# The ConvFFN of a hybrid decoder step in one pass, and in two passes with block products

## The chip, the cores and the metric

The kernel runs on one core of one Trainium2 chip. Time is device time in microseconds (us) of one execution. The core has five engines that work side by side, each through its own queue in order: TensorE (PE; its weight loads appear as PEld), VectorE (DVE), ScalarE (ACT), GpSimd (POOL) and SyncE (SP), which here issues nearly all DMA transfers. Working memory is SBUF, matmuls write into PSUM banks of 128 x 512 numbers, and large arrays lie in DRAM.

## What is computed

One layer of a decoder for 1024 prompt tokens and 8 x 8 sample tokens, in 32-bit floats, model width 1024. Attention of two kinds comes first; its output goes through W_o and is added to the residual h. Then comes the part that the change is about:

```python
def conv_ffn(n, prev, lw):                      # n = rmsnorm(h, g_ffn)
    a = n @ lw['ffn_w_gate']                    # 1024 x 2816
    c = n @ lw['ffn_w_up']                      # 1024 x 2816
    full = jnp.concatenate([prev, a], axis=1)   # two earlier rows
    conv = lw['ffn_conv_b'] + sum(w[j] * full[:, j:j + T] for j in range(3))
    y = (jax.nn.silu(conv) * c) @ lw['ffn_w_down']
    return y, full[:, -2:]
# h = h + y; then h = h + (p @ ple_w_proj) * sigmoid(rmsnorm(h, g_ple) @ ple_w_gate)
```

## The kernel before

Every product of 32-bit numbers is made of three matmuls (mm3): each operand is split into a high part (a cast on ScalarE) and a low part (a subtraction, on VectorE or GpSimd), and high x high, low x high and high x low are summed in PSUM. The helper for the split is at lines 115 to 117, for the three matmuls at lines 136 to 139, so many rows of the profile carry these line numbers.

A planner orders the instructions of each engine when the program is built. It takes them by their place in the source, but lets one that it thinks is ready go ahead of one that waits for data or for a free buffer. So instructions of a later place in the code can run early. Once the program is built the order on each engine is fixed.

Up to the FFN the work is a mixture of the prompt's dense stages and a stream over the sample's paged cache; wo_prompt (lines 1459 to 1484) starts the W_o product and loads the residual h (128 x 8 x 1024 in SBUF, 4 MB), and what is left of it follows at lines 1652 to 1662. There each token tile of 128 rows is normalised into a tile of its own (row_scale, xnorm, xn_tile), transposed by TensorE through PSUM and split into the tiles xg, in three groups of 384, 384 and 320 columns (256 prompt tokens and the 64 of the sample).

The FFN (lines 1682 to 1692) takes the 2816 columns in 22 chunks of 128, two at a time. ff_chunk multiplies the gate and the up weights of a chunk with all tokens: for each of the three groups of tokens 8 x 3 matmuls per matrix, with the activations moving (384, 384 and 320 columns). Then it copies the gate out of PSUM, runs the convolution on VectorE (lines 1597 to 1601), Silu on ScalarE, multiplies with up, and splits the result into sh and sl. After two chunks, down (lines 1380 to 1394) multiplies them with w_down for each token tile and adds the 512-column sums from PSUM to h in SBUF; down_sample (lines 1396 to 1408) does the same for the sample's 64 rows, whose high and low parts stand side by side in one 128-column operand. So h stays in SBUF for all of the FFN, and the product of gate and up never leaves SBUF.

During the last two chunks the tiles of h are normalised and transposed again (renormer), and the last stage (ple_unit, ple_sample) multiplies them with ple_w_gate and p with ple_w_proj, and writes the output.

## Time and profile before

| | us |
|---|---|
| median of 3 runs | 2309.12 |
| lowest, highest | 2305.56, 2311.49 |
| profiled execution, its own time | 2306.51 |
| its span (first to last instruction) | 2304.7 |
| TensorE busy | 2204.7 |
| VectorE busy | 1459.7 |
| ScalarE busy | 1243.1 |
| GpSimd busy | 951.0 |

The profile is that of the one execution that the last six rows tell of. Its page gives the busy time of each engine, then the span in 40 slices with the busy share of each in tenths, then the chain of work that ended last, and the costliest groups of instructions: line, engine, operation, written and read tiles, shape, count, then the group's busy time, the mean of one in ns, and the idle time of the engine before them with what ended it. In the table of stretches each engine has its busy time in the stretch, followed by the mean granted clock of TensorE, the DMA engines' busy share and GB/s. In the timeline a row has its start, its duration, engine, line and operation. Matmuls overlap each other, so their pace is read from the distance between starts, not from their durations.

### The profile page before, as it was taken

What the parts mean: (1) busy time and instruction counts of PE and PEld (TensorE: products, weight loads), DVE (VectorE), ACT (ScalarE), POOL (GpSimd) and SP (SyncE); (2) the same over time, 40 slices, a digit from 0 to 9 for tenths busy, and PEclk for the clock granted to TensorE, in tenths of its full rate; (3) what the DMA queues carried; (4) which work ended last, traced back from release to release, by engine and by line L of the source; (5) the groups of instructions that cost most, each with busy time, mean ns of one, the idle gap of its engine ahead of it and who ended that gap; (6) DMA issues with size and microseconds to landing.
All of it is one profiled execution on the core that took longest, in us unless ns stands there. A gap on an engine that the chain in (4) does not pass through costs nothing.

```text
span 2304.7 us, 37775 instructions
## 1 busy us (share of the span) xinstructions
PE 2204.7 (96%) x13855; PEld 1997.9 (87%) x13855; DVE 1459.7 (63%) x2386; ACT 1243.1 (54%) x3506; POOL 951.0 (41%) x1131
## 2 busy tenths in 40 slices
PE   7999999999999999998999869999999999999999
PEld 6889888878878888887887759999999999999999
DVE  4675775577798888887778665454444454444652
ACT  5666676777788888888557753221122221221531
POOL 5675677666777777776334540000000000000200
PEclk9899999999999999999999979999999999999999
DMA  5342334413242222215221112111111111111031
GB/s 179 118 133 94 103 111 145 125 49 104 73 112 64 59 64 63 58 43 174 78 68 61 46 33 78 46 46 43 32 55 47 46 46 37 46 47 32 29 116 40
DMA packets 173995, 169.84 MB, mean 74 GB/s; under 512 B 39022, under 2 KB 142931, under 8 KB 173811
## 3 DMA queue, kind: packets, MB, share of 16 engines
q1 hardware_dynamic: 161523, 125.47, 18.2%
q0 software_dynamic: 12288, 41.95, 5.9%
q8 instruction: 111, 1.82, 0.3%
q14 instruction: 73, 0.60, 0.1%
HBM read 140.81 MB, written 26.53 MB: 73 GB/s over the span
## 4 chain that ended last, share of the span: by engine, by line
PE 78%; ACT 7%; DVE 6%; POOL 3%; DMA 3%; issue 2%; SPq 0%; POOLq 0%; ACTq 0%; DVEq 0%
PE ps_gu L137 7%; PE ps_gu L139 7%; PE ps_gu L138 7%; PE ps_dn L137 5%; PE ps_dn L139 5%; PE ps_dn L138 5%; PE ks L137 4%; PE ks L139 4%; PE ks L138 4%; PE cpv L605 2%; ACT csq L542 2%; PE ctp L518 2%; PE ps_lt L276 2%; PE ps_pj L137 2%; DVE css L547 1%
## 5 line engine op out<-in xcount | busy, mean ns | idle before, releaser
L542 ACT ACTIVATE csq<-ks 128x256 f32<-128x256 f32 x1040 | 391.2, 400 | 103.0 <-PE ks L139 96.2
L547 DVE TENSOR_REDUCE css<-csq 128x16 f32<-128x1024 f32 (+1 forms) x264 | 315.9, 1197 | 70.8 <-ACT csq L542 67.8
L137 PE MATMUL ps_gu<-xh,guh 128*128 128x384 f32 (+1 forms) x1056 | 344.2, 326 | 0.9 <-ACT a L1591 0.7
L138 PE MATMUL ps_gu<-xl,guh 128*128 128x384 f32 (+1 forms) x1056 | 344.4, 326 | 0.0
L139 PE MATMUL ps_gu<-xh,gul 128*128 128x384 f32 (+1 forms) x1056 | 344.3, 326 | 0.0
L1391 DVE TENSOR_TENSOR h<-h,ps_dn 128x512 f32<-128x512 f32 x240 | 157.0, 684 | 88.8 <-PE ps_dn L139 88.4
L137 PEld LDWEIGHTS ps_gu<-xh,guh 128*128 128x128 f32 x1056 | 198.1, 188 | 1.8 <-ACT a L1591 0.8
L138 PEld LDWEIGHTS ps_gu<-xl,guh 128*128 128x128 f32 x1056 | 198.2, 188 | 0.5
L139 PEld LDWEIGHTS ps_gu<-xh,gul 128*128 128x128 f32 x1056 | 198.2, 188 | 0.0
L1602 POOL COPY cout<-a 128x2 f32<-128x2 f32 x22 | 11.1, 506 | 451.4 <-ACT a L1591 451.4
L137 PE MATMUL ps_dn<-wdh,sh 128*128 128x512 f32 x480 | 188.8, 396 | 1.6 <-DVE h L1391 0.9
L138 PE MATMUL ps_dn<-wdl,sh 128*128 128x512 f32 x480 | 188.0, 392 | 0.4 <-DVE wdl L117 0.4
L137 PE MATMUL ks<-mv1h,cTh 128*128 128x320 f32 (+1 forms) x520 | 168.4, 327 | 13.6 <-ACT cTh L116 7.0
L574 POOL TENSOR_TENSOR chl<-craw,chl 128x1024 fp32r<-128x1024 f32 x64 | 141.8, 2216 | 94.0 <-ACT chl L573 86.9
L139 PE MATMUL ps_dn<-wdh,sl 128*128 128x512 f32 x480 | 179.0, 391 | 0.0
L137 PE MATMUL ks<-mv0h,cTh 128*128 128x320 f32 (+1 forms) x520 | 169.3, 329 | 10.0 <-ACT csq L542 4.4
L116 ACT CAST guh<-stg 128x512 fp32r<-128x512 f32 x104 | 61.2, 620 | 174.1 <-PE ps_gu L138 136.6
L138 PE MATMUL ks<-mv1l,cTh 128*128 128x320 f32 (+1 forms) x520 | 152.4, 296 | 0.0
L138 PE MATMUL ks<-mv0l,cTh 128*128 128x320 f32 (+1 forms) x520 | 151.7, 294 | 0.0
L139 PE MATMUL ks<-mv1h,cTl 128*128 128x320 f32 (+1 forms) x520 | 143.9, 299 | 3.9 <-DVE cTl L117 3.9
L139 PE MATMUL ks<-mv0h,cTl 128*128 128x320 f32 (+1 forms) x520 | 145.0, 298 | 2.8 <-DVE cTl L117 2.7
L117 DVE TENSOR_TENSOR gul<-stg,guh 128x512 fp32r<-128x512 f32 x100 | 66.8, 696 | 121.0 <-ACT guh L116 120.5
(562 smaller groups left out, 6280.7 us busy)
## 6 DMA issues: line engine op xcount, KB each, us to landing
stage<-w_in SPq DMA_DIRECT2D x48, 256.0 KB
stg<-ffn_w_gate SPq DMA_DIRECT2D x44, 256.0 KB
stg<-ffn_w_up SPq DMA_DIRECT2D x44, 256.0 KB
stage<-ffn_w_down SPq DMA_DIRECT2D x44, 256.0 KB
oraw<-doT SPq DMA_DIRECT2D x16, 256.0 KB
stage<-w_o SPq DMA_DIRECT2D x16, 256.0 KB
h<-x_prompt SPq DMA_DIRECT2D x8, 512.0 KB
stg<-ple_w_gate SPq DMA_DIRECT2D x16, 256.0 KB
```

The costliest lines, as they stand in the source:

```text
L116: act.copy(hi, src)
L117: (lo_eng or dve).tensor_tensor(lo, src, hi.bitcast(F32), ALU.subtract)
L137: pe.matmul(ps, ah, bh, start=first, stop=False)
L138: pe.matmul(ps, ah, bl, start=False, stop=False)
L139: pe.matmul(ps, al, bh, start=False, stop=last)
L276: pe.matmul(ps, x, w, start=first, stop=last)
L518: pe.transpose(tp[:, i, :], craw[:, i, :], ident)
L542: act.activation(sq[:, f * 256:f * 256 + 256], ks[:, 0:256], AF.Square)
L547: dve.tensor_reduce(o.ss[:, g0 + i + 1 - n:g0 + i + 1, :].rearrange("p i h -> p (i h)"), sq2[:, :n].rearrange("p i (h n) -> p (i h) n", n= ...
L574: pool.tensor_tensor(ch[:, c0:c1, 128:256], src, ch[:, c0:c1, 0:128].bitcast(F32), ALU.subtract)
L605: pe.matmul(pv[:, 0:258], phl[:, i, :], o.ch[:, i, :], start=i == 0, stop=i == nt - 1)
L1391: dve.tensor_tensor(h[:, t, cs], h[:, t, cs], ps, ALU.add)
```

## The change

The FFN becomes two passes. In the first, all 22 chunks of gate, up, convolution and Silu are computed, and each chunk's product is written to DRAM (ds, 22 x 512 KB). In the second, the products come back as halves of 512 tokens, w_down as halves of 512 columns, and down adds to h by quarters. h itself is written to DRAM before it is normalised in place (dh, 4 MB) and loaded again between the passes. Its SBUF place is used by the first pass.

The first 768 tokens go another way through gate and up. Their transposed activations are four blocks: tokens 0 to 383 and 384 to 767, by the two halves of the 1024 inputs. The weights of a chunk are four blocks as well: gate and up, by the same halves (g0, g1, u0, u1). The eight block products that the gate and up of these tokens need are made out of seven products of sums and differences of blocks, as in Strassen's scheme: the activations' differences t1 to t4 are made once (turned_pair, from token tiles t and t + 3), the weights' s1 to s4 for each chunk (ff_weights, on GpSimd), and the seven products are put together by additions on VectorE and GpSimd in ff_chunk. The other 256 prompt tokens and the sample (320 columns) are multiplied as before, with the blocks g0, g1, u0, u1 (rest).

The sample's down is summed over all 22 chunks in two PSUM banks (acc_s) during the first pass, one chunk late, with w_down loaded and split for it there (sample_rows), and is added to the sample's residual once, between the passes. Pools of SBUF are opened and closed for each pass; the last stage's operands (p's slices, ple_w_proj) get a pool of their own, opened after the second pass.

The diff, cut to its core:

```diff
...
+    NP = 384
+    NR = T - 2 * NP + R
+    rx = opened("xhl", side="right")
+    xr = [z["xhl"].tile([P, 8, NR], F32R, name=f"xr{s}") for s in "hl"]
+    xb = {nm: [z["xhl"].tile([P, 4, NP], F32R, name=f"x{nm}{s}") for s in "hl"]
+          for nm in ("11", "21", "22", "t1", "t2", "t3", "t4")}
+    dh = [dram.tile([P if t < NT else R, D], F32, name=f"dh{t}") for t in range(NT + 1)]
+    ds = [dram.tile([P, T], F32, name=f"ds{f}") for f in range(NF)]
+
+    def normed(t):
+
+        row_scale(t)
+        x = hrows(t)
+        sp.dma_start(dh[t], x)
+        xnorm(t, x, pool if VIAP >> t & 1 else dve)
+
...
+    def turned_pair(t):
+        pc = slice(t * P, (t + 1) * P)
+        pt = {}
+        for nm, bank, rows, k0 in (("11", p2t, t, 0), ("12", pm, t + 3, 0), ("22", pm, t + 3, 4), ("21", p2t, t, 4)):
+            pt[nm] = bank([P, 4, P], "pt")
+            for k in range(4):
+                pe.transpose(pt[nm][:, k], hrows(rows)[:, (k0 + k) * P:(k0 + k + 1) * P], ident)
+        def quarter(tt, f):
+            return hrows(tt)[:, f * 512:f * 512 + 512].rearrange("p (k n) -> p k n", n=P)
+        def put(nm, src, eng):
+            split(*(x[:, :, pc] for x in xb[nm]), src, eng)
+        b11, t1, t2, t3 = quarter(t, 0), quarter(t, 1), quarter(t + 3, 0), quarter(t + 3, 1)
+        act.copy(b11, pt["11"])
+        dve.tensor_tensor(t1, pt["12"], b11, ALU.subtract)
+        dve.tensor_tensor(t2, pt["22"], t1, ALU.subtract)
+        put("22", pt["22"], dve)
+        put("11", b11, pool)
+        put("21", pt["21"], dve)
+        pool.tensor_tensor(t3, t2, b11, ALU.subtract)
+        dve.tensor_tensor(b11, pt["21"], t2, ALU.subtract)
+        put("t2", t2, pool)
+        put("t1", t1, dve)
+        put("t3", t3, pool)
+        put("t4", b11, dve)
+    def wstage():
+        return z["fw"].tile([P, 4, P], F32, tag="st", name="st", bufs=8)
+    def block(src, lo_eng):
+        hl = [z["fw"].tile([P, 4, P], F32R, tag="w" + s, name="w" + s, bufs=NWB) for s in "hl"]
+        split(*hl, src, lo_eng)
+        return hl
+    def ff_weights(f):
+        fs = slice(f * P, (f + 1) * P)
+        raw = []
+        for nm in ("ffn_w_gate", "ffn_w_up"):
+            for i in range(2):
+                r = wstage()
+                sp.dma_start(r, A[nm][0][i * 512:(i + 1) * 512, fs].rearrange("(k p) c -> p k c", p=P))
+                raw.append(r)
+        g0, g1, u0, u1 = raw
+        s1, s2, s3, s4 = (wstage() for _ in range(4))
+        w = wgu[f] = {}
+        w["g0"] = block(g0, dve)
+        w["g1"] = block(g1, dve)
+        pool.tensor_tensor(s1, u0, u1, ALU.add)
+        pool.tensor_tensor(s2, s1, g0, ALU.subtract)
+        w["s2"] = block(s2, dve)
+        w["s1"] = block(s1, dve)
+        pool.tensor_tensor(s4, g1, s2, ALU.subtract)
+        w["s4"] = block(s4, dve)
+        pool.tensor_tensor(s3, g0, u0, ALU.subtract)
+        w["s3"] = block(s3, dve)
+        w["u1"] = block(u1, pool)
+        w["u0"] = block(u0, pool)
+    def rest(w, names, bank):
+        ps = bank([P, 512], "ps_gu")
+        for i, nm in enumerate(names):
+            for k in range(4):
+                mm3(ps[:, :NR], w[nm][0][:, k], w[nm][1][:, k], xr[0][:, 4 * i + k], xr[1][:, 4 * i + k],
+                    i == k == 0, i == 1 and k == 3)
+        return ps
...
+    def sample_rows(f, half):
+        ss_ = chunks[f]
+        cs = slice(half * 512, half * 512 + 512)
+        raw = wstage().rearrange("p a b -> p (a b)")
+        sp.dma_start(raw, A["ffn_w_down"][0][f * P:(f + 1) * P, cs])
+        wd = [z["tp"].tile([P, 512], F32R, tag="wd" + s, name="wd" + s, bufs=2) for s in "hl"]
+        split(*wd, raw, dve)
+        if f == 0:
+            acc_s.append(p2t([P, 512], "ps_ds"))
+        for i in range(2):
+            pe.matmul(acc_s[half], ss_, wd[i], start=f == 0 and i == 0, stop=f == NF - 1 and i == 1)
+    def ff_chunk(f):
+        tp = z["tp"]
+        w = wgu.pop(f)
...
+        def product(wn, xn):
+            ps = both([P, 512], "ps_gu")[:, :NP]
+            for k in range(4):
+                mm3(ps, w[wn][0][:, k], w[wn][1][:, k], xb[xn][0][:, k], xb[xn][1][:, k], k == 0, k == 3)
+            return ps
+        pool.memset(a[:, 0:2], 0.0)
+        pool.tensor_copy(a_s[:, :, 0:2], prv[:, f])
+        m1, m2 = product("g0", "11"), product("g1", "21")
+        v, q, m5c = tmp("v"), tmp("q"), tmp("m5")
+        act.copy(v, m1)
+        dve.tensor_tensor(a[:, 2:2 + NP], m2, v, ALU.add)
+        pg = rest(w, ("g0", "g1"), both)
+        act.copy(a[:, 2 + 2 * NP:2 + T], pg[:, :T - 2 * NP])
+        act.copy(a_s[:, :, 2:10], pg[:, T - 2 * NP:NR].rearrange("p (b t) -> p b t", t=8))
+        if f + 1 < NF:
+            ff_weights(f + 1)
+        conv(0, NP)
+        act.activation(cv[:, 0:NP], cv[:, 0:NP], AF.Silu)
+        m6 = product("s2", "t2")
+        dve.tensor_tensor(v, m6, v, ALU.add)
+        if late:
+            sample_rows(late[0], 0)
+        m5 = product("s1", "t1")
+        act.copy(m5c, m5)
+        dve.tensor_tensor(q, m5, v, ALU.add)
+        m3 = product("s4", "22")
+        dve.tensor_tensor(a[:, 2 + NP:2 + 2 * NP], m3, q, ALU.add)
+        m7 = product("s3", "t3")
+        dve.tensor_tensor(v, m7, v, ALU.add)
+        pool.tensor_tensor(m5c, m5c, v, ALU.add)
+        if late:
+            sample_rows(late.pop(0), 1)
+        m4 = product("u1", "t4")
+        dve.tensor_tensor(v, m4, v, ALU.add)
+        pu = rest(w, ("u0", "u1"), both)
+        pool.tensor_tensor(cv[:, 0:NP], cv[:, 0:NP], v, ALU.mult)
+        conv(NP, T)
+        dve.tensor_scalar(cvs, a_s[:, :, 0:8], w3[0], w3[3], ALU.mult, ALU.add)
+        for j in (1, 2):
+            dve.scalar_tensor_tensor(cvs, a_s[:, :, j:j + 8], w3[j], cvs, ALU.mult, ALU.add)
+        pool.tensor_copy(cout[:, 0:2, f], a[:, T:T + 2])
+        pool.tensor_copy(cout[:, 2:18, f].rearrange("p (b j) -> p b j", j=2), a_s[:, :, 8:10])
+        act.activation(cv[:, NP:], cv[:, NP:], AF.Silu)
+        pool.tensor_tensor(cv[:, NP:2 * NP], cv[:, NP:2 * NP], m5c, ALU.mult)
+        dve.tensor_tensor(cv[:, 2 * NP:], cv[:, 2 * NP:], pu[:, :NR], ALU.mult)
+        sp.dma_start(ds[f], cv[:, 0:T])
+        ss_ = tp.tile([P, P], F32R, tag="ssm", name="ssm", bufs=2)
+        act.copy(ss_[:, 0:R], cv[:, T:])
+        dve.tensor_tensor(ss_[:, R:2 * R], cv[:, T:], ss_[:, 0:R].bitcast(F32), ALU.subtract)
+        chunks[f] = ss_
+        late.append(f)
...
+    order = (6, 7, 0, 3, 1, 4, 2, 5)
...
+    for _ in down((6, 7), pd, order, after):
+        pass
+    step(None)
+    step(None)
+    room["wf"].close()
+    room["hp"].close()
+    fw = opened("fw", side="right")
+    ff_weights(0)
+    rt = opened("tp")
+    for f in range(NF):
+        ff_chunk(f)
+    for half in range(2):
+        sample_rows(late[0], half)
+    rt.close()
+    fw.close()
+    rx.close()
...
+    def halves(tag, bufs=6):
+        return [z["wf"].tile([P, 512], F32R, tag=tag + s, name=tag + s, bufs=bufs) for s in "hl"]
+    def part(store, key, src, tag):
+        raw = stage([P, 512], F32, "raw")
+        sp.dma_start(raw, src)
+        hl = halves(tag)
+        split(*hl, raw)
+        store[key] = hl
+    sx, wx = {}, {}
+    def load_s(g, i):
+        for f in (g, g + 1):
+            part(sx, (f, i), ds[f][:, i * 512:i * 512 + 512], "s")
+    def load_w(g, j):
+        for f in (g, g + 1):
+            part(wx, (f, j), A["ffn_w_down"][0][f * P:(f + 1) * P, j * 512:j * 512 + 512], "w")
+    def quarter_down(g, i, j, after):
+        cs = slice(j * 512, j * 512 + 512)
+        for t in range(4 * i, 4 * i + 4):
+            tt = slice(t % 4 * P, t % 4 * P + P)
+            ps = both([P, 512], "ps_dn")
+            for n, f in enumerate((g, g + 1)):
+                s_, w_ = sx[f, i], wx[f, j]
+                mm3(ps, s_[0][:, tt], s_[1][:, tt], w_[0], w_[1], n == 0, n == 1)
+            dve.tensor_tensor(h[:, t, cs], h[:, t, cs], ps, ALU.add)
+            if after is not None:
+                after(t)
...
+    load_s(0, 0)
+    load_w(0, 0)
+    for t in range(NT + 1):
+        sp.dma_start(hrows(t), dh[t])
+    gain("g_ple")
+    for half in range(2):
+        fold_sample(acc_s[half], half)
+    stepq = renormer()
+    stepq(NT)
+    load_w(0, 1)
+    load_s(0, 1)
+    for g in range(0, NF, 2):
+        end = g == NF - 2
+        quarter_down(g, 0, 0, None)
+        if not end:
+            load_s(g + 2, 0)
+            load_w(g + 2, 0)
+        else:
+            wpl = ple_gate(0)
+        quarter_down(g, 0, 1, stepq if end else None)
+        quarter_down(g, 1, 0, None)
+        if not end:
+            load_w(g + 2, 1)
+            load_s(g + 2, 1)
+        else:
+            pass
+        quarter_down(g, 1, 1, stepq if end else None)
...
```

Before the first pass the remaining W_o product goes through the token tiles in the order shown, with each tile normalised after its sums and transposed two tiles later; hs, the sample's rows, come after tile 3. quarter_down has the activations as the stationary operand and 512 columns of w_down moving, as down had.

More of the change, by code (lines that the diff above doesn't have):

```diff
@@ L1377, in wo_chunk, with hrows, down @@
             split(sh[:, c0:c0 + 512], sl[:, c0:c0 + 512], raw)
-        chunks[c] = (sh, sl, oTg[:, c] if c < 4 else None) + wo_rows(c)
-    def down(grp, bank, after=None):
+        chunks[c] = (sh, sl, oTg[:, c] if c < 4 else None) + wdown(A["w_o"][0][c * P:(c + 1) * P, :])
+    def hrows(t):
+        return z["h"][:, t, :] if t < NT else z["hs"]
+    def down(grp, bank, order, after=None):
         h = z["h"]
-        for t in range(NT):
+        for t in order:
             tt = slice(t * P, (t + 1) * P)
@@ L1528, in turned @@
+    opened("fb")
+    rw = opened("wf")
+    chunks.clear()
     def turned(t, xn):
         rows = P if t < NT else R
-        if t == NT and "xss" in z:
-            transpose_split(p2t, xn, rows, lambda c0: tuple(z["xss"][:, c0:c0 + 4, s * R:(s + 1) * R] for s in range(2)))
+        if t == NT:
+            z["xss"] = xss = z["fb"].tile([P, 8, P], F32R, tag="xss", name="xss")
+            transpose_split(p2t, xn, rows, lambda c0: tuple(xss[:, c0:c0 + 4, s * R:(s + 1) * R] for s in range(2)))
```

249 lines of the change are left out of this document (101 added, 148 removed).

## The prediction

> **What bounds the kernel now.** I read the page first (span, busy shares, the slices), then stretches of the run side by side, then the pitch of single matmuls in the timeline, and the chain that ended last for where the FFN begins.
>
> ```profile
> span 2304.7 us, 37775 instructions
> PE 2204.7 (96%) x13855; PEld 1997.9 (87%) x13855; DVE 1459.7 (63%) x2386; ACT 1243.1 (54%) x3506; POOL 951.0 (41%) x1131
> ...
> PE   7999999999999999998999869999999999999999
> ```
>
> ```profile
> core 0: us, PE busy (x) PEld busy (x) DVE busy (x) ACT busy (x) POOL busy (x), PEclk, DMA share, GB/s
> 0.00:1072.00 1072.00, 1017.87 (x6821) 896.38 (x6821) 786.11 (x1343) 819.81 (x2495) 747.43 (x876) 0.99 0.32 95
> 1357.00:1377.00 20.00, 11.97 (x60) 9.98 (x58) 15.49 (x20) 10.96 (x20) 7.15 (x4) 0.58 0.17 53
> 1520.00:2080.00 560.00, 560.00 (x3100) 528.46 (x3099) 268.33 (x423) 119.74 (x208) 35.48 (x80) 1.00 0.15 46
> 2166.00:2305.00 139.00, 134.85 (x1127) 133.60 (x1125) 57.18 (x90) 40.41 (x77) 5.57 (x9) 1.00 0.21 65
> ```
>
> The fourth row of the table is the FFN in its steady state: TensorE busy 560.00 of 560 us at clock 1.00, while VectorE works 48% of the time, ScalarE 21%, GpSimd 6%. A busy TensorE may still be one that waits between overlapping matmuls, so I look at the starts.
>
> ```profile
> 1509.60 1.36 PE ps_dn L139 x6
> 1580.67 1.36 PE ps_dn L139 x6
> ```
>
> ```profile
> 1599.91 0.33 PE L137 MATMUL ps_gu<-xh,guh 128*128 128x384 f32 x1
> ...
> 1600.95 0.33 PE L137 MATMUL ps_gu<-xh,guh 128*128 128x384 f32 x1
> 1629.93 0.31 PE L138 MATMUL ps_gu<-xl,guh 128*128 128x320 f32 x1
> ...
> 1631.40 0.31 PE L139 MATMUL ps_gu<-xh,gul 128*128 128x320 f32 x1
> 1575.05 0.40 PE L137 MATMUL ps_dn<-wdh,sh 128*128 128x512 f32 x1
> ...
> 1576.43 0.39 PE L137 MATMUL ps_dn<-wdh,sh 128*128 128x512 f32 x1
> ```
>
> The chain passes the same place of two successive pairs of chunks 71.07 us apart. Six matmuls of 384 columns start within 1.04 us (0.173 each), ten of 320 within 1.47 (0.147), six of 512 within 1.38 (0.230). A pair of chunks holds 192, 96 and 104 of them: 33.2 + 14.1 + 23.9 = 71.2 us. So the period is the matmuls' own pitch with nothing between; only fewer or shorter matmuls shorten this stretch.
>
> **What is taken away.** With seven block products for eight, a chunk of 128 FFN columns has 84 matmuls of 384 columns instead of 96; the 320-column ones (the last 256 prompt tokens and the sample) stay 48, down stays 96 per pair, the sample's down 8 per pair. That is 24 fewer per pair, 264 over eleven pairs: 264 x 0.173 = **45.8 us off TensorE**. A chunk of the first pass is then 84 x 0.173 + 48 x 0.147 + 4 x 0.230 = 22.5 us, a pair in the second 96 x 0.230 = 22.1 us. The sample's fold into hs, eleven times today, now comes once; it stood beside a full TensorE and is worth nothing.
>
> **What is added inside the first pass**, beside 22.5 us of matmuls per chunk:
>
> ```profile
> L117 DVE TENSOR_TENSOR gul<-stg,guh 128x512 fp32r<-128x512 f32 x86 | 56.7, 689 | 119.6 <-ACT guh L116 119.2
> L1600 DVE SCALAR_TENSOR_TENSOR cv<-a,convT,cv 128x1024 f32<-128x1024 f32 x44 | 56.0, 1273 | 0.0
> L116 ACT CAST guh<-stg 128x512 fp32r<-128x512 f32 x86 | 50.5, 620 | 167.6 <-PE ps_gu L138 136.6 <-DMA stg<-ffn_w_gate 27.1 <-DMA stg<-ple_w_gate 3.6
> L1606 DVE TENSOR_TENSOR cv<-cv,ps_gu 128x384 f32<-128x384 f32 x44 | 24.2, 554 | 48.5 <-ACT cv L1604 26.7 <-PE ps_gu L139 21.8
> L1591 ACT COPY a<-ps_gu 128x384 f32<-128x384 f32 x44 | 20.9, 480 | 89.1 <-PE ps_gu L139 89.1
> L1597 DVE TENSOR_SCALAR cv<-a,convT 128x1024 f32<-128x1024 f32 x22 | 18.3, 830 | 9.3 <-ACT a L1591 9.2
> ```
>
> ```profile
> L564 POOL TENSOR_TENSOR sn<-sn,sr 128x512 f32<-128x512 f32 x42 | 55.4, 1319 | 1.0
> ```
>
> VectorE: six low parts of weight blocks and two of w_down, 8 x 0.689 = 5.5 us; six combining adds of 384 columns, 6 x 0.554 = 3.3; the convolution, cut in two for the prompt, by its columns today 0.83 + 2 x 1.27 = 3.4 and some 1.5 more for three more starts and the sample's; the last product and the sample's split about 0.8. Together 14.5 us, 64% of the chunk. GpSimd: six operations of 512 columns (four sums, two low parts) 6 x 1.32 = 7.9, three of 384 about 1.0 each by their columns, and the small copies of today: 11 to 12 us, 52%. ScalarE: ten casts 6.2, copies and Silu about 3: 9.2 us, 41%. None reaches 22.5, so TensorE should set the pace. A product may sit in its PSUM bank while five others run, since six banks turn: about five times 12 x 0.173 = 2.1 us, over 10 us. VectorE's queue holds six low parts and 1.7 us of convolution ahead of the next add, 5.8 us, within it. Weight blocks for the next chunk come into ten buffers of which a chunk fills eight; the later ones wait for this chunk's products, yet are wanted a chunk later. On SyncE the store of a chunk's product waits for its last multiplication, some 1 us behind the chunk's matmuls, with the loads for the chunk after next queued behind it; with the 2.6 us of a load (row below) they land some 4 us into the next chunk, 18 us before they are wanted. What stalls remain? Today none (the 560.00 row). The other bound is the first stretch, where VectorE, ScalarE and GpSimd are 73, 76 and 70% busy and TensorE loses 5%: 5% of 22 x 22.5 is 25 us. The loads lie between those rows, nearer to the steady one on ScalarE; I take 1%, **+5 us**.
>
> **The way into the FFN.**
>
> ```profile
> 1357.41 0.49 DVE late L614
> ...
> 1400.10 0.44 PE ps_gu L137
> ```
>
> The paged cache's last step ends at 1357.4, and only then are its SBUF and PSUM places free for the transposed activations. Until 1377 TensorE is busy 11.97 of 20 us at clock 0.58. The change puts three pairs of token tiles there: eight ScalarE operations (0.62), seven on VectorE (0.69) and four on GpSimd (1.3) for each pair, so 14.9, 14.5 and 15.8 us, where the same six tiles need 12 x 0.62 = 7.4 and 12 x 0.69 = 8.3 today. Against this, normalising writes in place and no longer needs a free tile, so it can go ahead of 1357 for all eight tiles. All three pairs have to be there before the first product, and the first chunk's weights wait for tiles of the W_o stage. Bounds: -8 (the idle part of the 20 us is used up) to +16 (the GpSimd chain comes whole on top). I take **+4 us**, what 7 us more per engine leave after the earlier normalising.
>
> **The seam between the passes** is new. Its prices:
>
> ```profile
> 1070.00:1075.00 5.00, 3.44 (x20) 2.94 (x21) 4.96 (x9) 4.01 (x13) 3.32 (x3) 1.00 1.00 405
> ```
>
> ```profile
> 2191.34 2.62 DMA stg<-ple_w_proj
> ```
>
> After the last product of chunk 21 come its multiplication, the sample's split and four matmuls, about 4 us; until then h's old place is held by the first pass's tiles. Then h returns, 8 x 0.524 MB = 4.2 MB, at the 405 GB/s that the first x_prompt load reached: 10.4 us, the first row tile after 1.3 + 2.6 us. Down's first quarter needs four halves split, about 3 us after the last product if their tiles lie free. Its sums can fill six banks (six times 6 x 0.230 = 8.3 us) before h is wanted, so h itself costs little; but w_down's second halves stand behind h in the program: if SyncE issues them there, they land near 4 + 10.4 + 2.6 + 1.3 = 18 us, and TensorE has used up the first quarter's 5.5 us by 8.5. The seam costs 3 to 15 us of idle TensorE and then some 2 us at a low clock (half the speed, as in the 0.58 row, for the first few us). Lower end 2, upper 20 with conv's tail; I take **+9**, the middle, as the planner orders by what it thinks is ready. In the second pass VectorE has 8 x 0.69 + 16 x 0.69 = 16.6 of 22.1 us, and traffic is 2.1 MB per pair, under 100 GB/s against 405: no stall taken.
>
> **The way into the last stage.** p's slices and w_proj are loaded only when the second pass's pool closes. Today the stage has TensorE busy 134.85 of 139.00 us, the largest single wait on the chain being the 2.62 us above. Two such loads in a row at worst, none at best: -2 to +6, I take **+2**.
>
> **Sum** on the profiled execution (2306.5 us; span 2304.7): 2306.5 - 45.8 + 5 + 4 + 9 + 2 = 2280.7. The median of the runs stands 2.6 us above that execution, so I forecast **2283 us**; with each seam at its own middle half the case runs from 2266 to 2300.
>
> **The rivals.**
>
> *The seams eat it.* Entry +16, seam +20, last stage +6 against 45.8, with 1% in the chunks: 2306.5 - 45.8 + 47 + 2.6 = 2310, no change. For it: every one of these is a chain of DMA, cast and subtraction on engines that issue in order; against: all at their worst ends at once. Chance 0.13.
>
> *VectorE and GpSimd get in each other's way.* This is the case of the other sign.
>
> ```profile
> 1341.20 2.18 POOL L574 TENSOR_TENSOR chl<-craw,chl 128x1024 fp32r<-128x1024 f32 x1 [2.49 <-ACT chl L573]
> ...
> 1362.11 5.25 POOL L1438 TENSOR_TENSOR xs<-xs,gb 128x1024 f32<-128x1024 f32 x2 [6.96 <-ACT xs L1435]
> ```
>
> ```profile
> 1341.36 0.69 DVE L589 TENSOR_TENSOR sn<-sn,mt 128x512 f32<-128x512 f32 x1 [0.52 <-PE mt L588]
> ...
> 1365.06 3.38 DVE L1432 SCALAR_TENSOR_TENSOR xs<-h,rs,gb 128x1024 f32<-128x1024 f32 x1
> ```
>
> For it: the last of these rows lasts 3.38 us where the same shape takes 1.27 in the convolution, and GpSimd is at work beside it. If the two engines shut each other out, a chunk of the first pass needs 14.5 + 11.7 = 26.2 us of them in turn, 3.7 over TensorE's 22.5: 22 x 3.7 = 81 us, 2283 - 5 + 81 = 2359 us. Against it: the 0.69 us row lies wholly inside a 2.18 us one of GpSimd and is no longer than elsewhere, and in the first 1072 us the two engines are busy 786 + 747 us together, which shutting out doesn't allow. The point from which it decides: the forecast gains 26 us, 1.2 us per chunk, so a chunk over 23.7 us turns the sign; late adds, banks that come free too late or weight blocks waiting for their buffers would come out in the same number. The Trainium skill, GPSIMD Engine Reference, Key points, speaks for this rival: GpSimd shares its SBUF interfaces with VectorE and contends with VectorE instructions that read two SBUF inputs, as nearly all of these do. By that rule taken whole the time would be the 2359 us above; the 0.69 us row doesn't agree, the 3.38 us row does. Chance of this rival in any strength that ends slower: 0.14.
>
> *Weight loads become the pace.*
>
> ```profile
> L137 PEld LDWEIGHTS ps_gu<-xh,guh 128*128 128x128 f32 x1056 | 198.1, 188 | 1.8 <-ACT a L1591 0.8
> ```
>
> A chunk of the first pass has 136 loads of 0.188 us, 25.6 us in a row, 3.1 more than its matmuls: 22 x 3.1 = 68 us, 2283 + 68 = 2351 us. But the 320-column matmuls already start every 0.147 us, each behind a load of 0.188, so loads overlap each other. The Trainium skill, Trainium Kernel Development and Optimization, Best Practices, would have one judge the distance to the limit by the busy share of weight loads, here 528.46 of 560 us and soon over the whole. By that rule nothing would be gained in the first pass; the 0.147 us pitch doesn't agree with it. Chance 0.02.
>
> *The seams cost nothing*, since the planner fills them: below 2266, at best 2306.5 - 45.8 - 8 + 2.6 = 2255. Chance 0.04. That fewer matmuls are saved than counted cannot be: the counts are the loops'.
>
> **How the numbers follow.** The forecast case has 0.67 and gives 2283 us. Three hundredths of the "seams eat it" case end just below 2302, so faster by over 0.3% (7 us, about what a measurement of this kernel can tell from no change) has 0.67 + 0.04 + 0.03 = 0.74; the other 0.10 of that case are no change; slower has 0.14 + 0.02 = 0.16. The range leaves out the two slow cases and a little at each end: 2264 to 2314 us.
>
> **What would show it.** Per pair of chunks the product matmuls of 384 columns number 168, and in the first pass the chain passes the same place every 22.5 to 22.8 us; in the second every 22.1. TensorE is busy in all but 1 to 3% of the first pass, with VectorE near 64%, GpSimd near 52%. Between the last product and the first of down TensorE idles 3 to 15 us, ended by a load of w_down or by h; the granted clock drops there and comes back. The first product starts between 1370 and 1393. I am wrong in the main step if a chunk takes over 23.7 us, above all if the sums on VectorE or GpSimd are longer than their rows here, and wrong in the seam if TensorE idles there for more than 20 us.

## The result, and the profile after

The changed kernel takes 2344.88 us (median of 4 runs, 2339.04 to 2349.83); beside it on the same chip the kernel before took 2310.14 (2305.56 to 2311.49). The ratio is 1.0153, 95% interval 1.0124 to 1.0182: slower by about 35 us. 2283 had been forecast, with a range from 2264 to 2314. The profiled execution took 2342.61 us, its span is 2340.9. The page after shows it at a glance: TensorE works 17.7 us less than before (2204.7), yet the span is 36.2 longer, with a dip in the slice of 1346 to 1404 us and one near 1960.

```profile
span 2340.9 us, 38650 instructions
...
PE 2187.0 (93%) x13591; PEld 1966.0 (84%) x13591; DVE 1655.8 (71%) x2623; ACT 1317.4 (56%) x3696; POOL 1210.5 (52%) x1315
...
PE   7999989999999999998999748999999997999999
```

The two traces, cut at the same four events, say where it went (starts of the instructions, us):

| stretch | before | after | difference |
|---|---|---|---|
| to the cache's last step (late, L614) | 1357.4 | 1358.5 | +1.1 |
| from there to the first product of gate and up | 19.6 | 48.3 | +28.7 |
| from there to the last matmul of down | 789.0 | 793.1 | +4.1 |
| from there to the end | 138.7 | 141.0 | +2.3 |

The third stretch was to be 45.8 us shorter. Side by side, the stretches after (columns as in the table of stretches before):

```profile
1357.00:1407.00 50.00, 22.75 (x105) 17.23 (x105) 32.15 (x45) 29.89 (x64) 28.48 (x24) 0.60 0.12 32
1460.00:1938.00 478.00, 460.43 (x2722) 447.19 (x2720) 347.36 (x498) 158.80 (x333) 258.06 (x252) 1.00 0.28 87
1938.00:1965.00 27.00, 13.02 (x37) 9.82 (x38) 11.42 (x19) 7.21 (x15) 0.86 (x2) 0.69 0.82 273
1965.00:2200.00 235.00, 235.00 (x1048) 194.00 (x1048) 170.96 (x263) 61.80 (x115) 5.74 (x12) 1.00 0.29 93
2200.00:2341.00 141.00, 135.08 (x1112) 134.01 (x1111) 54.56 (x86) 39.22 (x74) 6.60 (x7) 0.99 0.23 72
```

The second pass (fourth row) has TensorE busy without a gap, as forecast, and the last stage costs 2 us more, as forecast. The other three rows hold the loss: the entry, the first pass, where TensorE now waits, and the seam.

**In the first pass** the waits before matmuls and before SyncE's DMA issues (us in total, times, longest) name one place. In such a row, what waited stands left of the arrow and what ended the wait stands right of it.

```profile
PE ps_ds L1646 <- ACT wdh L116: 17.6, 17, 4.1
...
PE ps_ds L1646 <- DVE wdl L117: 3.6, 16, 0.2
```

```profile
SPq L1640 <- DVE wl L117: 261.9, 21, 14.3
```

TensorE waits for the split of w_down ahead of the sample's matmuls, once in most chunks. SyncE waits far longer ahead of the load of that w_down half: line 1640 takes a place in the ring of eight staging tiles (st), of which a chunk's four weight loads and its four sums s1 to s4 use all eight, so it can be issued only when VectorE has finished the low part of an old sum. One such chunk in the timeline:

```profile
1655.83 0.34 SPq L1640 DMA_DIRECT2D st<-ffn_w_down  x1
...
1658.45 0.62 ACT L116 CAST wdh<-st 128x512 fp32r<-128x512 f32 x1 [1.96 <-DMA st<-ffn_w_down]
...
1659.12 0.50 PE L1646 MATMUL ps_ds<-wdh,ssm 128*128 128x512 f32 x1 [1.74 <-ACT wdh L116]
```

The load is issued, its cast starts 2.6 us later, its matmul another 0.7 later. Counted against the pitch of 0.173, 0.147 and 0.230 us from one start to the next, all matmuls of the first pass start 34.9 us late in sum, 28.4 of it at line 1646. Two chunks 15 apart (start of their first product, fifth value) show the mean chunk as (1914.9 - 1551.3) / 15 = 24.2 us:

```profile
L137 PE MATMUL ps_gu<-x11h,wh x1: 338/338/338, 1551.3 to 1551.3; 128*128 128x384 f32 x1
L137 PE MATMUL ps_gu<-x11h,wh x1: 337/337/337, 1914.9 to 1914.9; 128*128 128x384 f32 x1
```

**At the seam** ScalarE's rows explain the longer wait of TensorE:

```profile
1942.70 1.22 ACT L116 CAST wh<-raw 128x512 fp32r<-128x512 f32 x2 [2.02 <-DMA raw<-ffn_w_down]
1959.20 0.58 ACT L1408 COPY fd<-ps_ds 64x512 f32<-64x512 f32 x1 [15.28 <-DVE hs L1409]
...
1960.46 1.16 ACT L116 CAST wh<-raw 128x512 fp32r<-128x512 f32 x2
```

```profile
1961.11 2.08 PE L137 MATMUL ps_dn<-wh,sh 128*128 128x512 f32 x4 [9.83 <-ACT wh L116]
```

The casts of w_down's second halves stand in ScalarE's queue behind the second copy of the sample's fold. That copy waits for the first half's addition to hs, and hs is loaded last, behind the eight tiles of h: in the chain its load takes from 1946.70 to 1958.38.

**At the entry** the first product starts right behind the first cast of a weight block, and that cast stands in ScalarE's queue behind the last cast of a block difference:

```profile
1405.61 0.62 ACT L116 CAST xt4h<-h 128x512 fp32r<-128x512 f32 x1
...
1406.13 1.14 ACT L116 CAST wh<-st 128x512 fp32r<-128x512 f32 x2
...
1406.80 0.69 PE L137 MATMUL ps_gu<-x11h,wh 128*128 128x384 f32 x1 [6.86 <-ACT wh L116]
```

The weights' loads had been issued at 1397.99, and the cast shows no wait for them. What is late is the pairs, and the squares of tiles 1, 4, 2 and 5 run only at 1376 to 1390, behind those of the sample.

Before, the first product did not wait for all tiles. Transposes of later token tiles (pt) stand among the products:

```profile
1376.99 0.43 PE L137 MATMUL ps_gu<-xh,guh 128*128 128x384 f32 x1
...
1382.06 0.60 PE L132 MATMUL pt<-ident,xs 128*128 128x128 f32 x4
```

### The profile page after: what moved, and what is told of

It is laid out like the page before. It is cut to its first block, busy times and chain, and to the rows that moved or that the text cites. A ratio compares the mean times of both kernels' runs of the same rounds, so it can differ in the third digit from the quotient of the medians.

```text
span 2340.9 us, 38650 instructions
## 1 busy us (share of the span) xinstructions
PE 2187.0 (93%) x13591; PEld 1966.0 (84%) x13591; DVE 1655.8 (71%) x2623; ACT 1317.4 (56%) x3696; POOL 1210.5 (52%) x1315
## 4 chain that ended last, share of the span: by engine, by line
PE 60%; POOL 10%; DMA 9%; DVE 8%; ACT 8%; issue 4%; SPq 1%; POOLq 0%; ACTq 0%; DVEq 0%
PE ps_dn L137 5%; PE ks L137 5%; PE ps_dn L139 5%; PE ps_dn L138 5%; PE ks L139 4%; PE ks L138 4%; DMA st<-ffn_w_down 3%; POOL wl L117 2%; PE cpv L605 2%; DMA st<-ffn_w_up 2%; PE ctp L518 2%; ACT csq L542 2%; PE ps_gu L137 2%; PE ps_gu L138 2%; PE ps_gu L139 2%
## 5 line engine op out<-in xcount | busy, mean ns | idle before, releaser
L137 PE MATMUL ps_dn<-wh,sh 128*128 128x512 f32 x352 | 139.1, 398 | 13.2 <-ACT wh L116 13.2
L139 PE MATMUL ps_dn<-wh,sl 128*128 128x512 f32 x352 | 138.1, 392 | 0.0
L138 PE MATMUL ps_dn<-wl,sh 128*128 128x512 f32 x352 | 138.1, 392 | 0.0
L117 DVE TENSOR_TENSOR wl<-st,wh 128x512 fp32r<-128x512 f32 x132 | 118.4, 911 | 14.8 <-ACT wh L116 14.8
L137 PEld LDWEIGHTS ks<-mv1h,cTh 128*128 128x128 f32 x520 | 100.2, 193 | 30.3 <-ACT sn L544 11.8
L117 DVE TENSOR_TENSOR cTl<-ctp,cTh 128x512 fp32r<-128x512 f32 (+1 forms) x136 | 90.0, 662 | 46.4 <-ACT cTh L116 45.4
L137 PEld LDWEIGHTS ks<-mv0h,cTh 128*128 128x128 f32 x520 | 98.8, 190 | 25.3 <-ACT csq L542 7.5
L544 ACT COPY sn<-ks 128x64 f32<-128x64 f32 x520 | 116.3, 224 | 0.0
L1276 POOL TENSOR_TENSOR pl<-p,ph 128x512 fp32r<-128x512 f32 (+1 forms) x96 | 97.2, 1018 | 34.8 <-DVE ph L1275 20.7
L116 ACT CAST wh<-st 128x512 fp32r<-128x512 f32 x176 | 102.8, 621 | 15.4 <-PE ps_gu L138 8.3
```

The lines of the kernel that those rows point to most:

```text
L116: act.copy(hi, src)
L117: (lo_eng or dve).tensor_tensor(lo, src, hi.bitcast(F32), ALU.subtract)
L137: pe.matmul(ps, ah, bh, start=first, stop=False)
L138: pe.matmul(ps, ah, bl, start=False, stop=False)
L139: pe.matmul(ps, al, bh, start=False, stop=last)
L544: act.copy(o.sn[:, g0 + i, :], ks[:, 256:320])
```

## The experiments

The theory after the result: the seven products save on TensorE what was counted, and three things of other kinds give it back: the staging ring in the first pass (some 25 to 30 us), the entry (some 25 more than forecast), the seam (some 10 more). The rivals: VectorE and GpSimd hold each other up, so that a chunk is slow whatever the ring; or the products are worth less than counted; or the losses belong to the two passes and not to the products. All ratios are against the kernel before, run beside it on the same chip; that chip was another one for e9_early than for the rest.

### The squares' scratch tile (e1_junk)

```diff
-            junk = z["junk"].tile([P, 512], BF16, tag="junk", name="junk")
+            junk = z["junk"].tile([P, 512], BF16, tag="junk" if t < NT else "junks", name="junk")
```

> The sample's scratch tile for the row sums gets a buffer of its own, so that normalising tiles 1, 4, 2 and 5 need not wait for the sample's rows. Theory A (one shared scratch buffer delays the entry): the squares of all eight tiles run before 1260 us, the first product moves from 1406.8 to 1385 to 1392 us, the whole is 15 to 22 us shorter (2323 to 2330). Rival C (the volume of the pairs' block sums on ScalarE, VectorE and GpSimd sets the entry): the squares move, the first product moves by less than 5 us, the whole by less than 5.

Measured: 2342.48 us, ratio 1.0147 (1.0130 to 1.0164), 2.4 us less than the changed kernel. The squares moved to before 1260 us, and the first product came 39.5 us after the cache's last step instead of 48.3, but that step came at 1362.9 instead of 1358.5. So the scratch tile did hold the squares back, and freeing it brought almost nothing: the two numbers of rival C hold (the first product moved by 4.4 us, the whole by 2.4). Its cause, the volume of the block sums, is put to the test by e6_plain. The step's time itself varies, 1356.2 to 1360.1 in four kernels here whose order up to it is the same, so one profile doesn't tell how much of the 4.4 us is the moved work and how much is chance; the median counts both. And what is left, 39.5 us against 19.6 before, is not the squares.

### A staging ring of its own for w_down (e2_stage)

```diff
-        raw = wstage().rearrange("p a b -> p (a b)")
+        raw = z["fw"].tile([P, 512], F32, tag="sw", name="sw", bufs=2)
...
-        wd = [z["tp"].tile([P, 512], F32R, tag="wd" + s, name="wd" + s, bufs=2) for s in "hl"]
+        wd = [z["tp"].tile([P, 512], F32R, tag="wd" + s, name="wd" + s, bufs=1) for s in "hl"]
```

> The staging tiles of the sample's w_down halves get a tag of their own with two buffers (the split tiles are cut from two to one, to make room), so they no longer queue for the ring of eight that the gate and up blocks use. Theory A (the staging ring holds w_down back): a chunk falls from 24.1 to 22.6 to 22.8 us, TensorE's wait at the sample's matmuls from 28 us in all to under 5, the whole is 25 to 33 us shorter (2312 to 2320). Rival B (VectorE and GpSimd stretch each other, and the chunk's chain is paced by them): a chunk stays above 23.7 us, TensorE waits elsewhere, the whole moves by less than 8 us.

Measured: 2320.78 us, ratio 1.0047 (1.0030 to 1.0064), 24 us less than the changed kernel, although the first product came 6 us later (the weight pool is 4 KB larger here, and SyncE waited 31.9 us for the last block difference before the first load; that the pool now reaches under h is inferred from this wait). The stretch of 20 chunks and two chunks 18 apart:

```profile
1462.00:1912.00 450.00, 450.00 (x2712) 446.50 (x2711) 364.30 (x496) 170.71 (x333) 271.28 (x254) 1.00 0.29 90
```

```profile
L137 PE MATMUL ps_gu<-x11h,wh x1: 337/337/337, 1483.8 to 1483.8; 128*128 128x384 f32 x1
L137 PE MATMUL ps_gu<-x11h,wh x1: 337/337/337, 1890.2 to 1890.2; 128*128 128x384 f32 x1
```

TensorE is busy 450.00 of 450 us and a chunk lasts (1890.2 - 1483.8) / 18 = 22.58 us, with the same work on VectorE (81% busy) and GpSimd (60%). So the shared ring was the cause of the late chunks; that VectorE and GpSimd by themselves hold the chunk up falls. A place in the ring came free only when VectorE had finished a low part, and such operations are longer beside GpSimd (below). How much shorter the ring's wait would be without that was not tried.

### Eight ordinary products (e6_plain)

The two passes as changed, with blocks 11, 21, 12, 22 and g0, g1, u0, u1 alone: no sums of weights, activations or products.

```diff
-          for nm in ("11", "21", "22", "t1", "t2", "t3", "t4")}
+          for nm in ("11", "21", "12", "22")}
...
-        s1, s2, s3, s4 = (wstage() for _ in range(4))
...
+        for nm, r in (("g0", g0), ("g1", g1), ("u0", u0), ("u1", u1)):
+            w[nm] = block(r, dve)
...
+        m1 = product(("g0", "g1"), ("11", "21"))
+        act.copy(a[:, 2:2 + NP], m1)
+        m2 = product(("g0", "g1"), ("12", "22"))
+        act.copy(a[:, 2 + NP:2 + 2 * NP], m2)
...
+        m3 = product(("u0", "u1"), ("11", "21"))
...
+        m4 = product(("u0", "u1"), ("12", "22"))
```

> The changed kernel's two passes with eight ordinary block products instead of seven: no sums of weight blocks, none of activations, none of products; order, staging ring and seam as in the changed kernel. Theory (the seven products are worth the 45.8 us that were counted, and what was lost stands beside them: the staging ring that the sums of the weight blocks fill, and the pair sums at the entry): a chunk of 24.6 us at a full TensorE with less than 5 us of stalls in the pass, the first product at about 1390 instead of 1407, the seam as before: 2344.9 + 45.8 - 30 - 16 = 2345 us (2335 to 2352). Rival (the stalls and the entry belong to the two passes themselves, whatever the products): 2344.9 + 45.8 = 2391 us. Second rival (the seven products are worth less than counted on TensorE): below 2330 us.

Measured: 2347.66 us, ratio 1.0166 (1.0144 to 1.0188), within 3 us of the changed kernel: against this kernel, the changed one gives back nearly all that its seven products save. Its first pass, and two chunks 18 apart:

```profile
1451.00:1943.00 492.00, 492.00 (x2958) 488.50 (x2957) 199.29 (x371) 123.56 (x251) 16.48 (x76) 1.00 0.26 79
```

```profile
L137 PE MATMUL ps_gu<-x11h,wh x1: 338/338/338, 1475.7 to 1475.7; 128*128 128x384 f32 x1
L137 PE MATMUL ps_gu<-x11h,wh x1: 338/338/338, 1919.0 to 1919.0; 128*128 128x384 f32 x1
```

A chunk lasts 24.63 us with no wait. Against 22.58 that is 2.05 per chunk, 45.1 us over 22: the saving that was counted as 45.8. The ring's waits are gone with the sums, so they belong to the products' sums and not to the two passes. The seam is as slow as in the changed kernel (starts 18.9 us late in sum, against 19.2). The entry disagrees with the expectation: 1400.1 instead of 1390, so of the 28.7 us some 8.5 (48.3 - 39.8 from the cache's last step, one profile each) belong to the block sums and to the weights' loads, which are issued from 1373.67 here; about 20 belong to the form of the entry itself.

### The order of the loads at the seam (e4_seam, e4_hs)

Both load hs ahead of h; e4_seam also moves the second quarters' loads ahead of h.

```diff
+    load_w(0, 1)
+    load_s(0, 1)
-    for t in range(NT + 1):
+    for t in (NT, *range(NT)):
         sp.dma_start(hrows(t), dh[t])
...
-    load_w(0, 1)
-    load_s(0, 1)
```

> Between the passes the sample's residual is loaded ahead of h, and the second halves of w_down and of the products are loaded ahead of h too. Theory A (ScalarE's queue is held by the sample's fold, which waits for the last of 4 MB, and the w_down halves are issued behind them): the 9.8 us wait inside the first quarter of down goes, TensorE waits about 5 us in all between the passes after 14, the whole is 7 to 10 us shorter. Rival D (h itself is late): the wait turns into one for h of 6 us or more, and the whole moves by less than 3 us.

> The changed kernel with one part of the seam edit alone: the sample's residual is loaded ahead of the eight tiles of h between the passes; the loads for the second quarter stay behind h. Theory (the 9.8 us wait at the seam is ScalarE's queue, held by the copy of the sample's fold, which waits for the residual): the wait goes or falls below 3 us and the time is within 4 us of the run with both moves, 2333 to 2337 us. Rival (the wait is the second quarter's loads behind 4 MB of h): the time stays at 2342 to 2347 us, with a wait of 7 us or more ended by a load of w_down or the products.

Measured: both moves together 2333.16 us, ratio 1.0104 (1.0088 to 1.0120), 11.7 us less than the changed kernel; hs alone 2342.97, ratio 1.0150 (1.0127 to 1.0172), 1.9 less. With hs alone the fold's copy comes at 1949.86, and ScalarE then idles for the load:

```profile
1949.86 0.58 ACT L1408 COPY fd<-ps_ds 64x512 f32<-64x512 f32 x1 [1.41 <-DVE hs L1409]
...
1960.69 1.26 ACT L116 CAST wh<-raw 128x512 fp32r<-128x512 f32 x2 [8.00 <-DMA raw<-ffn_w_down]
```

So the theory put to this run fell: the held queue let the cast go at 1960.46 in the changed kernel, and the loads behind h let it go at 1960.69 here. The two end together, and removing the first alone leaves the second. TensorE's waits in this run, at the seam:

```profile
PE pt L132 <- DVE xs L1428: 5.9, 1, 5.9
PE ps_dn L137 <- ACT wh L116: 4.8, 1, 4.8
```

The longer one is for the sample's normalised rows (xs), whose gain (gb) is loaded behind h as well, just ahead of w_down's second halves. In sum the starts are 17.5 us late. With both moved they are 8.3 us late instead of the changed kernel's 19.2. The other move alone, without hs, was not run.

### All three (e5_three)

The edits of e1_junk, e2_stage and e4_seam together.

> The three edits together. Theory A: they add up, 48 to 62 us shorter than the changed kernel, 2283 to 2297, which is 0.6 to 1.2% faster than the kernel before. Rivals B to D: what one edit frees is lost at the next wait, and the kernel stays above 2310 us.

Measured: 2307.77 us, ratio 0.9989 (0.9979 to 0.9998), 37 us less than the changed kernel. The expected 2283 to 2297 is missed, and the time doesn't stay above 2310 either, as the rivals had it. The medians of the singles sum up: 2344.9 - 2.4 - 24.1 - 11.7 = 2306.7. The stretches of the traces don't sum up one by one: from the first product to the last the time is 30.7 us shorter than in the changed kernel (30.5 in e2_stage), but from there to the last matmul of down only 5.4 (11.5 in e4_seam), and the starts at the seam are again 14.5 us late. Chunks last 22.57 us from the third on; the first product comes at 1403.7, 45.1 us after the cache's last step.

### The entry (e7_order, e8_nine, e9_early)

e7_order is the combination without the scratch tile's edit and with the pairs first:

```diff
-    order = (6, 7, 0, 3, 1, 4, 2, 5)
+    order = (0, 3, 1, 4, 2, 5, 6, 7)
...
-        if t == 3:
+        if t == 7:
             step(NT)
```

> The combination of the three edits, but with the tiles that go in pairs first in the order of the W_o product (0, 3, 1, 4, 2, 5, then 6, 7 and the sample), and the squares' junk tile shared again. Theory (the entry is set by the place of the pair's sums in the engines' queues: they stand behind the tiles 6 and 7 and the sample's chain, which need not be there for the first product): the first pair's sums start right after the cache's places come free at about 1360, the last block difference ends at 1385 to 1392 instead of 1398, the first product at 1388 to 1396 instead of 1404, and the time is 2307.8 - 10 = 2298 us (2293 to 2302). Rival (the volume of the transposes, casts and sums after the cache sets it, whatever their order): the last difference still ends at 1397 to 1402 and the time stays at 2305 to 2310 us. A second rival: the tiles 6, 7 and the sample, now last, are late for the 320-column products of the first chunks, and the first chunk lasts 5 us or more longer; then 2305 us or more as well, but with the first product early.

Measured: 2309.54 us, ratio 1.0005 (0.9996 to 1.0015). The last block difference came 34.0 us after the cache's last step instead of 39.3 in e5_three, but that step came at 1365.0 instead of 1358.6, above all those named so far, and the first product at 1406.2. The rival's time stands, though not its reason: the differences do end sooner after the step, but the step comes later by 6.4 us in this profile, and the way from the last product to the last matmul of down is 3.8 us longer than in e5_three. Whether the moved work delays the step was not tried.

e8_nine adds one edit, nine buffers for weight blocks instead of ten.

```diff
-NWB = 10
+NWB = 9
```

> As the run with the pairs first, and nine buffers for weight blocks instead of ten, so that the first pass's weight pool is no larger than in the changed kernel and need not wait for the places of h that the last normalised tiles use. Theory (the first chunk's weights wait for the last block difference only because the two added staging tiles made the pool reach into h's place): the first weight load is issued 8 us or more ahead of the last block difference, the first product comes 2 to 8 us earlier than with ten buffers, and the steady chunk stays at 22.6 us, since eight blocks are used by a chunk: 2290 to 2296 us. Rival (the ninth buffer is too few, so that the next chunk's first weight blocks wait for this chunk's last products): chunks of 23 us or more, +10 us and over, 2305 us or more.

Measured: 2307.57 us, ratio 0.9990 (0.9978 to 1.0002). Chunks stay at 22.57 us, so nine buffers do; but the first weight load is still issued at 1406.3, after the last difference at 1402.9, now behind the transposes of the last tiles. Counted from the cache's last step, at 1368.9 here, the load comes 37.4 us later, as in e7_order. The theory about the pool's size fell for this order: without the 4 KB the load waits as long. Nine buffers with the order of e5_three were not tried.

e9_early is e5_three with the first turn of the weight buffers begun five places on, nothing else in any engine's order being changed:

```diff
     def ff_weights(f):
+        if f == 0:
+            for _ in range(5):
+                for s in "hl":
+                    z["fw"].tile([P, 4, P], F32R, tag="w" + s, name="w" + s, bufs=NWB)
```

> The combination of the three edits, with nothing changed in any engine's order, but the first chunk's weight loads and buffers placed so that they don't lie under h: five buffers of the ring of ten, those under h, are passed over at the first turn. Theory (between the last block difference and the first product stand a weight load and a cast that only the place of the buffers holds back): the first weight load is issued at about 1376 instead of 1400, right behind the sample's store, the first cast of a weight block stands right behind the last cast of a block difference, the first product comes at 1398 to 1400 instead of 1403.7, and the time is 2303 us (2301 to 2306). Rival (the loads run beside the pair sums and the sample's tail and slow them, or the cast is late for another reason): the first product stays at 1402 to 1405 and the time at 2306 to 2310 us.

Measured: 2301.52 us, ratio 0.9962 (0.9947 to 0.9976): faster than the kernel before by 8.4 us, and the only kernel here that is faster by over 0.3%.

```profile
1380.21 1.00 SPq L1607 DMA_DIRECT2D st<-ffn_w_gate  x2
```

```profile
1403.01 1.14 ACT L116 CAST wh<-st 128x512 fp32r<-128x512 f32 x2 [1.70 <-DVE xt4l L117]
```

The loads go 20 us earlier, the first product comes 41.2 us after the cache's last step instead of 45.1, and the second chunk lasts 22.57 us instead of 24.04. In this profile the cache's last step came 3.8 us later than in e5_three with the same order up to there. So the first product, at 1403.7, misses the expected 1398 to 1400, but counted from that step it comes as expected (39.4 to 41.4). The first cast still waits 1.7 us for the last block difference; its place seems to lie under h still. The two spans are alike (2301.2 and 2301.5); the gain shows in the medians, whose intervals against the kernel before don't overlap. Of the 0.27% between the two ratios, some 6 us, the traces show the 3.9 us of the entry; the rest is not traced.

What keeps even this kernel from more: its entry still takes 41.2 us against 19.6 before, and the starts at its seam are 15.2 us late. Together they take most of what the products save.

## Why the prediction was wrong

Right was the largest term, what the products save on TensorE; the sign of the sum was wrong. A chunk was put at 22.5 us and lasts 22.58 when nothing holds it; 45.8 us were put on the seven products and 45.1 are measured. The second pass runs without a stall, and the last stage costs 2.3 us against a forecast of 2. The sum failed in three terms, all of them waits:

- **"Stalls in the first pass, 1%, +5 us"**: 34.9 measured. The step that failed is the one that checked the buffers. It counted the ten buffers of weight blocks, of which eight are used, and the loads for the next chunk, 18 us ahead of need. It did not count the eight staging tiles, which loads and sums fill, nor that the loads of the sample's w_down take their turn in that ring with matmuls of the same chunk behind them. e2_stage removes it and brings 24 us although its entry is 6 us later.
- **"The way into the FFN, +4 us", bounds -8 to +16**: 28.7 measured, outside the bounds. The price was the difference of busy time per engine, 7 us. But the entry is a chain that crosses TensorE, ScalarE, VectorE and GpSimd for each pair, and the products cannot start before its end. Before, they could, as the rows at 1376.99 and 1382.06 show. e6_plain shows that most of the loss, about 20 us, comes without any block sum. That normalising would "go ahead of 1357 for all eight tiles" failed as well, by the shared scratch tile, but e1_junk shows that freeing it was worth 2 us, not the loss. That these 20 us are the wait for the whole chain is argued from the order of the queues: no run let the products start before all pairs were there. Why the chain needs 40 us and not fewer is not settled further; its parts were not taken out one by one.
- **"The seam, +9 us"**: starts late by 19.2, near the upper bound of 20. Named rightly were w_down's second halves behind h; not seen was that ScalarE's queue is also held by the sample's fold, whose residual is loaded last. With the residual alone moved the starts are still 17.5 us late; both moved bring 11.7 us of time.

With the measured sizes the sum is -45.8 + 34.9 + 28.7 + 19.2 + 2.3 + 1.1 = +40.4 against 36.2 in the spans. The 4 us between lie in the stretch of the products: before, 57 transposes hold TensorE for 7.5 us there (from each start to the next), after, 24 hold it for 2.3. Against these 5.2 us less stand eight more of the sample's matmuls, 8 x 0.230 = 1.8 us; that leaves 3.4 of the 4.

**"The seams eat it"** came true in its mechanism and beyond its price: entry, seam and last stage cost 28.7 + 19.2 + 2.3 = 50.2 us, where the rival had 42 at all their worst ends. The first pass comes on top.

**The rival that came true only in its number** is that of VectorE and GpSimd. Its point of decision was 23.7 us per chunk, the chunk took 24.1 over the whole pass ((1937.3 - 1406.8) / 22), and the sign turned, by a cause that the prediction had listed only among others that would give the same number (weight blocks waiting for their buffers). That the number fits this rival is luck. The mechanism itself is real, and the matmuls hide it: e6_plain (GpSimd 3% busy) and e2_stage (60%) between 1462 and 1905 us, by shape (busy us, mean ns):

```profile
L117 DVE TENSOR_TENSOR wl<-st,wh 128x512 fp32r<-128x512 f32 x70 | 48.5, 692 | 119.4 <-ACT wh L116 119.1
L1627 DVE SCALAR_TENSOR_TENSOR cv<-a,convT,cv 128x640 f32<-128x640 f32 x36 | 31.5, 874 | 0.0
...
L1665 DVE TENSOR_TENSOR cv<-cv,ps_gu 128x384 f32<-128x384 f32 x18 | 10.0, 554 | 56.2 <-PE ps_gu L139 56.2
```

```profile
L117 DVE TENSOR_TENSOR wl<-st,wh 128x512 fp32r<-128x512 f32 x114 | 107.1, 940 | 38.3 <-ACT wh L116 38.3
L1660 DVE SCALAR_TENSOR_TENSOR cv<-a,convT,cv 128x640 f32<-128x640 f32 x38 | 60.7, 1597 | 0.7
...
L1711 DVE TENSOR_TENSOR ssm<-cv,ssm 128x64 fp32r<-128x64 f32 x20 | 19.8, 990 | 0.3 <-ACT ssm L1710 0.3
...
L1682 DVE TENSOR_TENSOR v<-ps_gu,v 128x384 f32<-128x384 f32 x20 | 11.1, 557 | 0.9 <-PE ps_gu L139 0.6
...
L1691 DVE TENSOR_TENSOR v<-ps_gu,v 128x384 f32<-128x384 f32 x19 | 10.4, 545 | 0.0
```

So VectorE's 14.5 us per chunk of the forecast became 364.30 / 450.00 x 22.58 = 18.3. Operations with both inputs in SBUF are stretched from 692 to 940 ns and from 874 to 1597, and the sample's split (ssm) takes 990. Those with one input in PSUM stay at 545 to 557. Of these the additions at line 1691 are the test, since each of the 19 lies wholly beside a GpSimd operation; none of the 20 at line 1682 has one beside it. The prediction's price of this rival, 26.2 us in turn, counted all of VectorE's work. Counted with the undisturbed means, only six low parts, two of w_down and the convolution have two SBUF inputs: 6 x 0.69 + 2 x 0.69 + 2 x (0.87 + 0.62 + 0.27) = 9.0 us (0.2 more with the sample's split), and with GpSimd's 11.7 of the forecast that makes 20.7, below the chunk's 22.58. So by this estimate even turns would be hidden here. The Trainium skill, SBUF — State Buffer, section Who interferes with whom, says just this: with two SBUF inputs a VectorE instruction contends with GpSimd reads, with at most one it does not (outside two-port modes); the rows above agree. The prediction held a row of 0.69 us beside GpSimd against this rival (sn<-sn,mt). Its mt lies in PSUM, so that row could not show the effect, and not nearly all of VectorE's operations read two SBUF inputs, as the prediction says.

**Weight loads as the pace** fell: in e2_stage they are busy 446.50 of 450.00 us, and the chunk still goes by the matmuls' pitch.

## What to carry to other kernels

A saving on the busiest engine is kept only if every buffer ring, queue place and load order around it is counted for the new traffic: here 45 us were saved as computed, and 24 of them hung on one ring of eight tiles in which a short-lived load took its turn behind long-lived ones. Where a change replaces "start when the first operands are there" by "start when all are there", price the whole chain across the engines, not the added busy time of each. When two causes end a wait almost together, remove both before judging either: here one alone brought 1.9 us and both brought 11.7.

## What the runs showed of the hardware

GpSimd's cost to VectorE hangs on where VectorE reads. Row by row in e2_stage, a low part of 512 columns from SBUF takes 0.69 us when no long GpSimd operation lies beside it (60 of 114) and 1.22 on average when one does (54 of 114, at most 1.60); with PSUM as one input the 384-column addition takes 0.54 to 0.56 in both cases. The convolution's first step over 640 columns (line 1658, one SBUF array and two numbers per row) mostly keeps its time: 17 of 19 beside GpSimd took 0.61 to 0.80, but two took 1.57 and 1.74, and no run here says why. And a 0.26 MB load of w_down issued behind 4 MB of h took 9.6 us from its issue to its cast (1951.06 to 1960.69 in e4_hs), where the w_down load of the timeline above took 2.6.
